# Moving the background's turn behind the copy or sum of each product, and gated splits behind the last copy and sum

## The chip, the cores and the metric

The kernel runs on one core of one Trainium2 chip. The metric is the device time of one execution in microseconds (us); lower is better. A core has engines with a queue of instructions each: TensorE (PE in the profile) multiplies matrices, VectorE (DVE) and ScalarE (ACT) work on tiles, GpSimd (POOL) does the same more slowly, and SyncE (SP) here only issues transfers between the memory of the chip and on-chip tiles. The engines run beside one another and wait for each other through semaphores; within one engine, instructions run in the order in which they stand in its queue.

## The reference

One decoder block over 2048 positions of width 1024, in float32. Its mixer has two parts, gated linear attention and a short gated convolution, between one input and one output projection; then comes a gated FFN of width 2816.

```python
h = rmsnorm(x, norm1_g[l])
proj = h @ w_in[l]
...
o = gla_chunked(q, k, v, log_a)
o = rmsnorm(o, gla_norm_g[l]).astype(x.dtype)
o = o * jax.nn.silu(p_g.reshape(bsz, seq, GLA_HEADS, GLA_DV))
...
u = c_c * c_h
o_conv = c_b * causal_depthwise_conv(u, conv_w[l])
mixed = jnp.concatenate([o_gla, o_conv], axis=-1) @ w_out[l]
x = x + mixed
h2 = rmsnorm(x, norm2_g[l])
ffn = (jax.nn.silu(h2 @ w_ffn_gate[l]) * (h2 @ w_ffn_up[l])) @ w_ffn_down[l]
x = x + ffn
return rmsnorm(x, norm_f_g)
```

## The kernel before

The positions are worked on in two halves of 1024, each half two blocks of 512. Almost all of TensorE's time goes into products of 128 x 512 tiles. A `unit` computes a two by two block of output tiles (c11, c12, c21, c22) from a two by two block of weights and of operands with seven products in place of eight, in the manner of Strassen. The names in `PRODUCTS` are pairs of a weight combination (A11, S1, S2, A12, S3, S4, A22) and an operand combination (B11, T1, T2, B21, T3, B22, T4), and below they are P0 to P6 in this order. Each product runs over four slices of the contraction (two or three in FFN down), and each slice takes three matmuls (L460, L461, L462), because a float32 value is split into a rounded high part (an ACT copy, L193) and the rest (a DVE subtraction, L194): high times high, high times low, low times high. A product is so 12 matmuls as a rule. The weights arrive as `raw`, are combined on POOL or DVE (L435), and split into `wq`; operands arrive as `op`.

The products of a unit share accumulators. P0 goes into bank `oa` and is copied to c11 (`copied`, L500, ACT); P1 goes into `ob` and is copied to c22; P2 is added into `oa` and copied to c12; P3 has a bank of its own and is added to c11 (`plus`, L489, DVE); P4 goes on in `oa` and is added to c22; P5 goes on in `ob` and is added to c12; P6 ends `oa`, which is c21. So the next product in a bank cannot start before the copy or the sum of the one before it has read the bank. In FFN down after its first unit all copies are sums into `y`.

Beside these products runs a "background": generators with the work of other parts (operands of the next stage, the gated linear attention, splits of gated values in FFN up), of which one step is traced at a turn. A turn is a call of `tick` (L271). It counts `pace`; on even counts, or while `hurry` is set, it traces one step of the background; `steady`, `hasty` and `ahead` add steps at some counts; while `ordered` is set, in the first units, it does nothing. In `mul` the turn comes after the product's matmuls (L481) and so ahead of its copy or sum in the program.

What stands in the program is not yet the order of an engine's queue: a scheduler places instructions by the program's order and by when their operands are to be ready (`TileContext` at L1634, with a simulated timeline). `behind(marks)` (L158) adds an edge: what is issued within it stands behind the marked instructions where they are on its own engine. `last_out` holds the last copy of L500 and `last_plus` the last sum of L489; the row statistics (`row_stats`, L545) and `kept` (L352) use these marks already.

In FFN up, a pair of units gives a gate and a value, whose product (DVE, L1310) is a gated value (c or sg in the profile's names, t for the differences POOL makes of them). `split_later` (L1321) is put into the background for them: values in `WHOLE` are stored as they are, the others are split by `store_split` (L1331) into `so`, of which there are three buffers, and stored for FFN down. Transfers of the next stage's operands (`op`, L148) and stores (L151) go through SP's one queue: `in_proj(1)`, the second half's input projection, loads its operands from `siB` and `siT`, which the first half's background makes and stores as pairs `hi` and `lo`, and the attention of the first half loads `kq`, `ee`, `vt` and `gt` in the same queue.

Of the kernel before, what the change touches and what calls it, by code (L numbers as in the profile page):

```python
# [53 lines left out]
def tile_hymba_block(ctx, tc, x, xt, win, wa, wgu, wout, wffn, wdown, wdown_first, small, out):  # L54
# [83 lines left out]
    def bank(name="mm"):  # L138
        return ps.tile([P, PB], F32, name=name, tag="mm")

    def tt(name):
        return tp.tile([P, PB], F32, name=name, tag="t")
# [7 lines left out]
    def store(dst, src):  # L150
        return nc.sync.dma_start(dst, src)  # L151

    last_hi, last_lo, raw_loads = [], [], []
    last_out = []
    unit_splits, unsplit, held, last_plus, with_marks = [], [], [], [], []

    @contextmanager
    def behind(marks):  # L158

        with ExitStack() as stack:  # L160
            for m in marks:
                stack.enter_context(tc.issue_after(m.ins))
            yield
# [3 lines left out]
    def queued(eng, issue):  # L167

        with behind([tails[eng]] if eng in tails else []):
            tails[eng] = issue()  # L170
        return tails[eng]
# [18 lines left out]
    def split(src, hi, lo):  # L190
        if ordered:
            return split_in_order(src, hi, lo)
        last_hi[:] = [act.activation(hi, src, AF.Copy)]  # L193
        last_lo[:] = [dve.tensor_tensor(lo, src, hi.bitcast(F32), ALU.subtract)]  # L194
        return last_lo[0]
# [67 lines left out]
    def step():  # L263
        while background:
            try:
                next(background[0])
                return
            except StopIteration:
                background.pop(0)

    def tick():  # L271
        pace[0] += 1
        if ordered:
            return
        if pace[0] % 2 == 0 or hurry:
            step()
            if steady and pace[0] % 4 == 0:
                step()
        elif hasty and pace[0] % 4 == 3:
            step()  # L280
        elif ahead and pace[0] % 4 == 1:
            next(ahead[0], None)
# [114 lines left out]
    def weight_quarter(src):  # L397

        n = src.shape[-1]
        if halves:  # L400
            h = halves.pop()
        else:
            h = wqp.tile([P, 2, PB], F32R, name="wq", tag="wq")
            if n == PB // 2:
                halves.append(h[:, :, n:])
            h = h[:, :, 0:n]
        split(src, h[:, 0, :], h[:, 1, :])
        catch_up()
        return h
# [8 lines left out]
    def unit_weights(src, raw=None, between=(), eng=pool):  # L418
        raw = raw_weights(src) if raw is None else raw
        between = iter(between)  # L420

        def others():
            for job in next(between, ()):
                job()

        n = src.shape[-1]
        a11, a12, a22, a21 = [raw[:, i, :] for i in range(4)]
        s1 = rawp.tile([P, PB], F32, name="s1", tag="s1", bufs=1)[:, 0:n]
        w = {"A11": weight_quarter(a11)}

        def mix(*args):
            if ordered:
                queued(dve, lambda: dve.tensor_tensor(*args))
            else:
                eng.tensor_tensor(*args)  # L435

        mix(s1, a21, a22, ALU.add)
        mix(a21, a11, a21, ALU.subtract)
        mix(a11, s1, a11, ALU.subtract)
        w["S1"] = weight_quarter(s1)  # L440
        others()
        w["S2"] = weight_quarter(a11)
        others()
        w["A12"] = weight_quarter(a12)
        others()
        w["S3"] = weight_quarter(a21)
        others()
        mix(a12, a12, a11, ALU.subtract)
        w["S4"] = weight_quarter(a12)
        others()  # L450
        w["A22"] = a22 if ordered else weight_quarter(a22)
        halves.clear()
        return w

    def product_step(o, w, op, k, first):
        n = len(op)
        c = slice(k * P, (k + 1) * P)
        wh, wl = w[:, 0, c], w[:, 1, c]
        xh, xl = op[k][:, 0, :], op[k][:, 1, :]
        pe.matmul(o[:], wh, xh, start=first and k == 0, stop=False, skip_group_check=True)  # L460
        pe.matmul(o[:], wh, xl, start=False, stop=False, skip_group_check=True)  # L461
        return pe.matmul(o[:], wl, xh, start=False, stop=k == n - 1, skip_group_check=True)  # L462

    def unit(src, ops, into=None, onto=None, raw=None, between=(), rest=None, eng=pool):

        w = unit_weights(src, raw, between, eng)
        unit_splits[:] = last_hi + last_lo
        with behind(unit_splits):  # L470
            for y, o in unsplit:
                split(y[:], o[:, 0, :], o[:, 1, :])
        unsplit.clear()

        def mul(i, o=None):
            first = o is None
            o = bank() if first else o
            n, m = PRODUCTS[i]
            for k in range(len(ops[m])):
                product_step(o, w[n], ops[m], k, first)  # L480
            tick()  # L481
            return o

        def plus(t, o):
            if ordered:
                queued(dve, lambda: dve.tensor_tensor(t[:], o[:], t[:], ALU.add))
            else:
                with behind(held if rest is not None else []):
                    last_plus[:] = [dve.tensor_tensor(t[:], o[:], t[:], ALU.add)]  # L489
            return t  # L490

        def then():
            if rest is not None:
                next(rest)

        def copied(name, o, at):
            if onto is not None:
                return plus(onto[at], o)
            t = tt(name) if into is None else into[at]
            last_out[:] = [act.activation(t[:], o[:], AF.Copy)]  # L500
            return t


        oa = mul(0)
        c11 = copied("c11", oa, (0, 0))
        ob = mul(1)
        c22 = copied("c22", ob, (1, 1))
        mul(2, oa)
        c12 = copied("c12", oa, (0, 1))
        o = mul(3)  # L510
        then()
        plus(c11, o)
        mul(4, oa)
        then()
        plus(c22, oa)
        if rest is not None:
            next(rest, None)
            w["A22"] = weight_quarter(w["A22"])
            held[:] = last_hi + last_lo
            ordered.clear()  # L520
        mul(5, ob)
        plus(c12, ob)
        mul(6, oa)
        if into is not None or onto is not None:
            copied("c21", oa, (1, 0))
        return [(0, 0, c11, False), (1, 1, c22, False), (0, 1, c12, False), (1, 0, oa, True)]

    def settled(c, in_psum):
# [480 lines left out]
    def in_proj(half, ops, raw=None, between=(), rest=None):  # L1009
        def units():  # L1010
            if half == 0:
                yield unit(win[2], ops, raw=raw, between=between, rest=rest)
            for u in range(0 if half else 3, 12):
                yield unit(win[u], ops, eng=pool if half else dve)
# [289 lines left out]
    def ffn_up(half, ops):  # L1304
        for m in range(NF // 2):
            us = unit(wffn[2 * m], ops)
            sg = {(r, j): silu(c, p) for r, j, c, p in us}
            for r, j, c, _ in unit(wffn[2 * m + 1], ops):
                s = sg[r, j]
                dve.tensor_tensor(s[:], c[:], s[:], ALU.mult)  # L1310
            b11, b12, b21, b22 = [sg[r, j] for r in range(2) for j in range(2)]
            t1, t2, t3, t4 = [bt(n) for n in ("t1", "t2", "t3", "t4")]
            for y, p, q in ((t1, b12, b11), (t2, b22, t1), (t3, b22, b12), (t4, b21, t2)):
                pool.tensor_tensor(y[:], p[:], q[:], ALU.subtract)
            values = [("B11", b11), ("B21", b21), ("B22", b22)]
            if half == 1 and m >= LAST_GROUP:
                values.append(("B12", b12))
            values += [("T1", t1), ("T2", t2), ("T3", t3), ("T4", t4)]
            background.insert(0, split_later(s_act[half][m], values))

    def split_later(dst, values):  # L1321

        for n, y in values:
            if n in WHOLE:
                store(dst[n][:], y[:])
        for n, y in values:
            if n not in WHOLE:
                store_split(dst[n], y)
                yield

    def store_split(dst, y):  # L1331
        o = bx[1].tile([P, 2, PB], F32R, name="so", tag="so")
        split(y[:], o[:, 0, :], o[:, 1, :])
        store(dst[:], o[:].bitcast(F32))
# [304 lines left out]
```

## Time and profile before

| | us |
|---|---|
| median of 3 runs | 2064.49 |
| the runs | 2064.49, 2065.36, 2061.48 |
| profiled execution | 2061.84 |
| its span | 2060.1 |
| TensorE busy | 2023.8 |
| DVE, ACT, POOL busy | 1429.7, 971.3, 770.3 |

All times inside the profile are counted from the start of the span. The stages of the span are these: the first half's input projection up to about 240 us; the second half's, with the first half's attention in the background, up to about 560; the output projections, which have matmuls of lines of their own (L1201 to L1204), up to about 785; FFN up of the first half to about 1190, FFN down to about 1430; then FFN up of the second half to about 1835 and FFN down to the end.

A group of the profile gives busy time, mean duration, and the idle time of its engine just before it with what ended it; the view of waits gives the same idle time by waiting line and releasing line (total, times, longest). In the timeline a row gives the start, the duration, engine, line, operation, output and inputs, and in brackets the idle time before it. A row of the view of windows gives the busy time of PE, weight load, DVE, ACT and POOL in a stretch, then the granted clock of TensorE (1 is full speed), the busy share of the DMA engines and GB/s.

### The profile page before, as it was taken

The page shows a single profiled execution, that of the slowest core. Times are in us where ns is not written, and L with a number is a line of the kernel's source. Part 1 is how long each engine was busy: PE and PEld are TensorE (multiplying, and loading weights), DVE is VectorE, ACT ScalarE, POOL GpSimd, SP SyncE. Part 2 cuts the span into 40 slices and gives each one's busy share as a digit, 9 for nine tenths or more (in the row PEclk, how much of TensorE's full clock was granted, in tenths as well). Part 3 has the DMA queues.
Part 4 walks back from the last instruction along what each step waited for, and adds up shares of the span by engine and source line. Part 5 has one row for each costly group of instructions (what it writes and reads, how often), then busy time and mean ns, then how long its engine had stood idle before and what let it go on. Part 6 is the DMA issues. An engine that isn't in the chain of part 4 may idle for free.

```text
span 2060.1 us, 27151 instructions
## 1 busy us (share of the span) xinstructions
PE 2023.8 (98%) x9271; PEld 1663.5 (81%) x9271; DVE 1429.7 (69%) x2185; ACT 971.3 (47%) x1932; POOL 770.3 (37%) x566
## 2 busy tenths in 40 slices
PE   9999999999999999999999999999999999999997
PEld 8778878887888887888888888787888888888786
DVE  7878976559743786677675677766766666667774
ACT  6765455765542344444444552335434443453344
POOL 0000022113102574464564345533644554434544
PEclk9999999999999999999999999999999999999998
DMA  7356796425686873555454676576444434486653
GB/s 260 124 188 212 285 313 189 130 82 166 225 273 228 319 260 128 199 181 206 160 180 147 234 278 248 184 272 260 162 170 164 169 148 169 173 314 222 235 216 126
DMA packets 189739, 422.54 MB, mean 205 GB/s; under 512 B 19904, under 2 KB 65184, under 8 KB 180128
## 3 DMA queue, kind: packets, MB, share of 16 engines
q1 hardware_dynamic: 189600, 420.81, 57.8%
q8 instruction: 73, 1.20, 0.2%
q14 instruction: 66, 0.54, 0.1%
HBM read 276.02 MB, written 144.70 MB: 204 GB/s over the span
## 4 chain that ended last, share of the span: by engine, by line
PE 82%; DVE 8%; DMA 5%; ACT 2%; issue 2%; POOL 1%; SPq 0%; DVEq 0%; ACTq 0%; POOLq 0%
PE mm L460 24%; PE mm L462 23%; PE mm L461 23%; PE mm L1201 2%; PE mm L1202 2%; PE mm L1204 2%; DVE wq L194 1%; DVE op L194 1%; DMA raw<-in_win_dram 1%; DMA op<-shT 1%; DMA op<-siT 1%; DVE h L882 1%; PE a_ps L958 1%; PE mm L744 1%; PE mm L746 1%
## 5 line engine op out<-in xcount | busy, mean ns | idle before, releaser
L460 PE MATMUL mm<-op,wq 128*128 128x512 f32 x2467 | 964.0, 393 | 20.1 <-ACT c L500 8.4
L461 PE MATMUL mm<-op,wq 128*128 128x512 f32 x2467 | 961.2, 390 | 0.4 <-DVE op L194 0.4
L462 PE MATMUL mm<-op,wq 128*128 128x512 f32 x2467 | 950.8, 391 | 1.3 <-DVE wq L194 1.0
L194 DVE TENSOR_TENSOR wq<-raw,wq 128x512 fp32r<-128x512 f32 (+2 forms) x612 | 488.3, 803 | 243.6 <-ACT wq L193 240.8
L193 ACT ACTIVATE wq<-raw 128x512 fp32r<-128x512 f32 (+2 forms) x612 | 355.8, 587 | 590.5 <-PE mm L462 447.5
L460 PEld LDWEIGHTS mm<-op,wq 128*128 128x128 f32 x2467 | 463.9, 188 | 125.6 <-ACT c L500 11.8
L462 PEld LDWEIGHTS mm<-op,wq 128*128 128x128 f32 x2467 | 463.8, 188 | 101.8 <-DVE wq L194 4.6
L461 PEld LDWEIGHTS mm<-op,wq 128*128 128x128 f32 x2467 | 464.1, 188 | 96.0 <-DVE op L194 2.1
L435 POOL TENSOR_TENSOR s<-raw 128x512 f32<-128x512 f32 (+2 forms) x87 | 114.4, 1315 | 449.2 <-DVE wq L194 299.0
L435 POOL TENSOR_TENSOR raw<-raw 128x512 f32<-128x512 f32 (+2 forms) x174 | 227.1, 1310 | 135.9 <-DVE wq L194 126.6
L435 POOL TENSOR_TENSOR raw<-s,raw 128x512 f32<-128x512 f32 (+2 forms) x87 | 111.3, 1280 | 410.3 <-DVE wq L194 372.6
L489 DVE TENSOR_TENSOR y<-mm,y 128x512 f32<-128x512 f32 x185 | 126.8, 687 | 80.0 <-PE mm L462 79.8
L489 DVE TENSOR_TENSOR c<-mm,c 128x512 f32<-128x512 f32 x196 | 134.7, 687 | 68.4 <-PE mm L462 66.3
L1183 POOL TENSOR_TENSOR ssx<-ssx,q 128x512 f32<-128x512 f32 x52 | 76.3, 1482 | 162.3 <-ACT q L1182 162.0
L500 ACT ACTIVATE c<-mm 128x512 f32<-128x512 f32 x198 | 115.7, 587 | 19.5 <-PE mm L462 16.6
L1201 PE MATMUL mm<-op,wq 128*128 128x512 f32 x256 | 100.9, 395 | 0.0
L1202 PE MATMUL mm<-op,wq 128*128 128x512 f32 x256 | 99.9, 390 | 0.0
L193 ACT ACTIVATE wq<-s 128x512 fp32r<-128x512 f32 (+2 forms) x96 | 56.2, 585 | 84.0 <-PE mm L462 79.9
L194 DVE TENSOR_TENSOR wq<-s,wq 128x512 fp32r<-128x512 f32 (+2 forms) x96 | 82.4, 858 | 2.8 <-ACT wq L193 2.1
L194 DVE TENSOR_TENSOR op<-op 128x512 fp32r<-128x512 f32 x94 | 76.6, 844 | 8.7 <-ACT op L193 8.6
L1204 PE MATMUL mm<-op,wq 128*128 128x512 f32 x256 | 80.2, 391 | 0.0
L1396 POOL TENSOR_TENSOR y<-x,y 128x512 f32<-128x512 f32 x32 | 53.7, 1679 | 45.3 <-DVE y L489 45.3
(232 smaller groups left out, 1847.0 us busy)
## 6 DMA issues: line engine op xcount, KB each, us to landing
raw<-in_wffn_dram SPq DMA_DIRECT2D x44, 1024.0 KB, 6.0
sa_B<-so SPq DMA_DIRECT2D x47, 512.0 KB, 4.3
op<-sa_B SPq DMA_DIRECT2D x47, 512.0 KB, 6.9
raw<-in_win_dram SPq DMA_DIRECT2D x22, 1024.0 KB, 5.4
sa_T<-so SPq DMA_DIRECT2D x44, 512.0 KB, 4.5
op<-sa_T SPq DMA_DIRECT2D x44, 512.0 KB, 6.7
raw<-in_wdown_dram SPq DMA_DIRECT2D x24, 768.0 KB, 6.1
sx<-y SPq DMA_DIRECT2D x48, 256.0 KB, 4.0
```

What stands on the lines that cost most here:

```text
L193: last_hi[:] = [act.activation(hi, src, AF.Copy)]
L194: last_lo[:] = [dve.tensor_tensor(lo, src, hi.bitcast(F32), ALU.subtract)]
L435: eng.tensor_tensor(*args)
L460: pe.matmul(o[:], wh, xh, start=first and k == 0, stop=False, skip_group_check=True)
L461: pe.matmul(o[:], wh, xl, start=False, stop=False, skip_group_check=True)
L462: return pe.matmul(o[:], wl, xh, start=False, stop=k == n - 1, skip_group_check=True)
L489: last_plus[:] = [dve.tensor_tensor(t[:], o[:], t[:], ALU.add)]
L500: last_out[:] = [act.activation(t[:], o[:], AF.Copy)]
L1183: pool.tensor_tensor(ssq[:], ssq[:], q[:], ALU.add)
L1201: pe.matmul(o[e, j][:], wh, m[:, 0, :], start=k == 0, stop=False)
L1202: pe.matmul(o[e, j][:], wh, m[:, 1, :], start=False, stop=False)
L1204: pe.matmul(o[e, j][:], wl, ops[k][j][:, 0, :], start=False, stop=k == KD - 1)
```

## The change

In `unit`, `mul` no longer calls `tick`; each of the seven products has its turn after its copy or sum, and after P6 also where nothing is copied. The number of turns of a unit and their counting are the same. In `split_later`, the split and store of a gated value now stand behind the last copy and the last sum issued at that moment: its ACT copy behind the last ACT copy of L500, its DVE subtraction behind the last DVE sum of L489. No arithmetic is changed.

```diff
@@ unit
             for k in range(len(ops[m])):
                 product_step(o, w[n], ops[m], k, first)
-            tick()
             return o
...
         oa = mul(0)
         c11 = copied("c11", oa, (0, 0))
+        tick()
         ob = mul(1)
         c22 = copied("c22", ob, (1, 1))
+        tick()
         mul(2, oa)
         c12 = copied("c12", oa, (0, 1))
+        tick()
         o = mul(3)
         then()
         plus(c11, o)
+        tick()
         mul(4, oa)
         then()
         plus(c22, oa)
+        tick()
...
         mul(5, ob)
         plus(c12, ob)
+        tick()
         mul(6, oa)
         if into is not None or onto is not None:
             copied("c21", oa, (1, 0))
+        tick()
@@ split_later
             if n not in WHOLE:
-                store_split(dst[n], y)
+                with behind(last_out + last_plus):
+                    store_split(dst[n], y)
                 yield
```

Built, the changed kernel has as many instructions on each engine as before, but for two activation table loads fewer on ACT. TensorE's products stand in another order in a few regions only.

## The prediction

> **What bounds the kernel now.** I read the page first (span, busy times, the chain that ended last, the groups), then the waits of TensorE, then stretches of the timeline around each of its longest waits.
>
> ```profile
> span 2060.1 us, 27151 instructions
> PE 2023.8 (98%) x9271; PEld 1663.5 (81%) x9271; DVE 1429.7 (69%) x2185; ACT 971.3 (47%) x1932; POOL 770.3 (37%) x566
> ...
> PE 82%; DVE 8%; DMA 5%; ACT 2%; issue 2%; POOL 1%; SPq 0%; DVEq 0%; ACTq 0%; POOLq 0%
> ...
> L460 PE MATMUL mm<-op,wq 128*128 128x512 f32 x2467 | 964.0, 393 | 20.1 <-ACT c L500 8.4
> ```
>
> TensorE bounds it: busy 2023.8 of 2060.1 us, so 36.3 us is all that any reordering can win. The start of a product (L460) carries 20.1 us of that idle time. The waits of TensorE say for whom:
>
> ```profile
> PE mm L460 <- ACT c L500: 8.4, 7, 2.1
> PE mm L460 <- DVE c L489: 3.9, 5, 1.6
> PE mm L460 <- ACT wq L193: 2.2, 2, 1.8
> PE mm L460 <- DVE y L489: 2.2, 4, 1.2
> ```
>
> Seven waits for a copy and nine for a sum, 14.5 us together, are what this change can reach: the copy (L500, ACT) and the sum (L489, DVE) must be done before the next product that writes the same bank. Only the places where a background instruction stands between are touched, though. Following these sixteen waits through the order of instructions of both kernels, I find the same instructions ahead in three of the copies and seven of the sums: operand splits, a table load and gate work of the foreground, which no turn of the background places. So most of the 36.3 us stays.
>
> **The change, part by part.** It adds and removes no instruction by itself. A turn of the background now comes after the copy or sum of its product, not before it, 7 turns a unit as before, and the scheduler's order of instructions changes in some regions only. Copies with a background instruction directly ahead fall from 28 to 8 and sums from 44 to 37; elsewhere TensorE's order of products is unchanged, in particular through most of the FFN. I take each region.
>
> *FFN up, steady.* 21 of the 28 copies stood behind a split of a gated value (so, L193) that waits for DVE:
>
> ```profile
> ACT so L193 <- DVE c L1310: 35.1, 22, 2.8
> ```
>
> ACT idles 35.1 us there, but TensorE waits in only one of those units, because the copy has a whole product (12 matmuls at 0.23 us, 2.7 us) to be done in. That unit is this one:
>
> ```profile
> 834.32 0.68 DVE L1310 TENSOR_TENSOR c<-c,c 128x512 f32<-128x512 f32 x1
> 835.03 0.63 ACT L193 ACTIVATE so<-c 128x512 fp32r<-128x512 f32 x1 [2.75 <-DVE c L1310]
> 835.57 0.58 ACT L500 ACTIVATE c<-mm 128x512 f32<-128x512 f32 x1
> 836.20 0.50 PE L460 MATMUL mm<-op,wq 128*128 128x512 f32 x1 [1.19 <-ACT c L500]
> ```
>
> The copy could have run 2.75 us earlier; after, it stands ahead of the split: **-1.2** (bounds -1.2 and 0, if another split takes the place). The other 21 cost 0 now and 0 after. The split's two edges to the last copy and sum delay the stores of the gated values by at most about a product, 2.7 us; these are read back only a group later in FFN down, except the last group's, taken next.
>
> *First unit of FFN down, both halves.* A DVE sum stands behind three subtractions of `so`:
>
> ```profile
> 1837.40 0.91 DVE L194 TENSOR_TENSOR so<-sg,so 128x512 fp32r<-128x512 f32 x1
> 1838.24 0.68 DVE L194 TENSOR_TENSOR so<-c,so 128x512 fp32r<-128x512 f32 x1
> 1838.84 0.68 DVE L194 TENSOR_TENSOR so<-t,so 128x512 fp32r<-128x512 f32 x1
> 1839.44 0.68 DVE L489 TENSOR_TENSOR y<-mm,y 128x512 f32<-128x512 f32 x1
> 1840.17 0.50 PE L460 MATMUL mm<-op,wq 128*128 128x512 f32 x1 [1.20 <-DVE y L489]
> ...
> 1197.60 0.50 PE L460 MATMUL mm<-op,wq 128*128 128x512 f32 x1 [0.69 <-DVE y L489]
> ```
>
> After, the subtractions are spread between sums. Waits of 0.69 and 1.20 go; I leave 0.2 of each for the one subtraction that may remain ahead: **-1.5** (bounds -1.9 and 0). A copy in the second half's FFN up (0.7 us at 1503) has two more matmuls as cover, 0.46 us: **-0.4** (bounds -0.7 and 0).
>
> *First half's input projection, 100 to 135 us.* The largest single item:
>
> ```profile
> 120.78 1.28 ACT L1005 ACT_TABLE_LOAD   x1
> ...
> 124.03 0.61 ACT L193 ACTIVATE wq<-raw 128x512 fp32r<-128x512 f32 x1
> ...
> 122.45 0.39 PE L462 MATMUL mm<-op,wq 128*128 128x512 f32 x1
> 124.69 0.50 PE L460 MATMUL mm<-op,wq 128*128 128x512 f32 x1 [1.85 <-ACT wq L193]
> ...
> 126.77 0.63 PE L460 MATMUL mm<-op,wq 128*128 128x512 f32 x1
> 127.19 0.63 PE L461 MATMUL mm<-op,wq 128*128 128x512 f32 x1
> ...
> 126.00:130.00 4.00, 4.00 (x14) 3.25 (x13) 3.40 (x9) 2.13 (x4) 0.00 (x0) 0.57 0.34 131
> ```
>
> A weight split stands behind the table load and the squares of the row statistics, TensorE waits 1.85 us, and right after it the granted clock is 0.57 over four microseconds: matmuls 0.42 us apart for about 8 of them, 0.2 us each too much, 1.6 us. After, this table load is gone (two of ACT's loads go, 1.28 us each; ACT is 47% busy, so they count only here), the split comes earlier, and both go: -3.5. But two pairs of dependent products, P4 and P6 of a unit, then follow each other in one bank with nothing between. The nearest row of such a pair:
>
> ```profile
> 488.05 0.39 PE L1127 MATMUL o_ps<-carry,kq 128*128 128x128 f32 x2
> 488.48 0.68 DVE L489 TENSOR_TENSOR c<-mm,c 128x512 f32<-128x512 f32 x1
> 489.21 0.50 PE L460 MATMUL mm<-op,wq 128*128 128x512 f32 x1 [0.78 <-DVE c L489]
> ```
>
> End of the last matmul (0.39 after its start), 0.05 to the sum, 0.68, 0.05 to the matmul, less the normal 0.23 step: 0.95 us each, +1.9. Net **-1.6** (bounds -3.5, if the pairs find other work between, and +1.9, if the split is still late).
>
> *195 to 225 us.* DVE is the full engine here:
>
> ```profile
> 180.00:225.00 45.00, 44.71 (x198) 36.73 (x197) 44.96 (x74) 22.97 (x45) 0.00 (x0) 1.00 0.72 241
> ```
>
> DVE is busy 44.96 of 45.00 us, and TensorE still idles only 0.3. Two new pairs, P2 and P4, come with two matmuls between: 0.95 - 0.45 = 0.5 each; the 0.3 us wait for a copy goes: **+0.7** (bounds -0.3, and +3.2 with each pair at the longest wait for such a sum, 1.6).
>
> *Where the second half's input projection begins.* SP's queue and transfers set this stretch:
>
> ```profile
> 243.09 1.68 SPq L148 DMA_DIRECT2D op<-siB  x3
> 244.83 0.42 SPq L148 DMA_DIRECT2D kq<-sk  x1
> 246.06 0.32 SPq L151 DMA_DIRECT2D siB<-lo  x1
> 246.66 0.32 SPq L151 DMA_DIRECT2D siT<-t  x1
> ...
> 242.00:249.00 7.00, 7.00 (x32) 5.82 (x31) 7.00 (x10) 2.60 (x5) 3.30 (x2) 1.00 0.78 240
> 249.00:278.00 29.00, 26.89 (x118) 21.64 (x117) 21.93 (x37) 15.61 (x31) 2.89 (x2) 1.00 1.01 383
> ...
> 273.45 1.25 ACT L193 ACTIVATE op<-op 128x512 fp32r<-128x512 f32 x2 [1.90 <-DMA op<-siT]
> ...
> 275.75 1.14 ACT L193 ACTIVATE op<-op 128x512 fp32r<-128x512 f32 x2
> 276.79 0.58 ACT L500 ACTIVATE c<-mm 128x512 f32<-128x512 f32 x1
> ...
> 277.42 0.50 PE L460 MATMUL mm<-op,wq 128*128 128x512 f32 x1 [2.11 <-ACT c L500]
> ```
>
> The DMA engines are full (share 1.01) from 249 to 278, and an operand split waits on a transfer. After, the stores of `siB` and `siT` and more small `kq` loads (0.4 us of queue each) stand in SP's queue ahead of the first three operand loads, which so start after 246.66, not at 243.09: 3.6 us later. The engines' free share before 249 takes 1.5 of it back (7 us at 1 - 0.78), which leaves +2.1; one more operand split (0.57 each in the row of two) ahead of the copy at 276.79 gives +0.5. The wait of 2.1 us becomes 4.7; whether the clock halves behind it is even, since 1.85 us was followed by it and 2.11 us was not: half of 1.6, +0.8. **+3.4** (bounds 0, if the other loads in flight hide it, and +5.8: 3.6, 0.6 and 1.6).
>
> Sum: -1.2 - 1.5 - 0.4 - 1.6 + 0.7 + 3.4 = -0.6 us. The profiled execution took 2061.84 us and the median of the runs is 2064.49, 2.65 above it, within their spread of 3.9 us; on the median the forecast is **2063.9 us**.
>
> The Trainium skill, "TensorE: Matmul & The Clock Gate", Part 1, says that the clock falls to half after an idle activity window of about 3.4 us, on windows that run freely, and its part on oscillation that gaps up to that length are harmless. The trace differs: 1.85 us of waiting was enough once. By the rule, the halving at 126 would not belong to that wait.
>
> **The rivals.** *DVE's full stretch gives way (slower, 0.20).* Between 180 and 240 the sums of some 20 products pass a DVE queue without a gap. If the new order lets a weight subtraction of 1.4 us slip ahead of a sum whose product has no cover, TensorE waits that long. It decides against the change from four such sums (4 x 1.4 = 5.6, against the -1.3 of the other terms); with six, 8.4 - 1.3 = +7.1, 2071.6. Against it: the count of sums behind the background falls. *The operand loads come as late as their issue (slower, 0.10).* 5.8 in place of 3.4, and the next product also waits for its operand, 3.6 more; with the -4.0 of the other terms +5.4, 2069.9. It decides from 8.1 us at this place. The full DMA share speaks for it, the idle share before 249 against. *Nothing new is late (faster, 0.22).* The loads hide (0), the pairs find cover (-3.5, -0.3), and the other three go whole: -3.5 - 0.3 - 1.2 - 1.9 - 0.7 = -7.6, 2056.9; with the pairs at half, 2058.5. *The change doesn't act (0.08):* the large waits have foreground work ahead and the terms cancel, 2064.5. *The halving is no child of the wait (0.08):* the 1.6 stays at some other place and falls due in full behind 4.7 us of waiting: -0.6 + 1.6 + 0.8 = +1.8, 2066.3; that the 2.11 us wait went without it speaks for it. This is the time by the skill's rule above.
>
> **How the numbers follow.** The forecast itself has 0.32. About 0.2%, 4.1 us, is what a measurement of this kernel can tell. Faster by that: most of the third rival and a little of the forecast's own spread, 0.24. Slower: most of the first two and a little of the rest, 0.29. Within: 0.47. For the range I leave out the far ends of the first and third rival and take 2057.5 to 2070.5; the forecast's own range is 2060 to 2068.
>
> **What would show it.** Right: ACT's waits of `so` for L1310 no longer precede a copy; no TensorE wait at 835, and about 0.2 at 1197 and 1840; the clock at 1.0 from 123 to 130, with two new waits of about 1 us for DVE c L489 between 100 and 135; the first operand loads of the second half issued after 246.7 and waits of some 4 to 5 us near 277; table loads of L540 and L1005 at 6 and 0. Wrong: new waits for L489 in 180 to 240 above 1 us in all, a wait near 277 that didn't grow or grew past 6, or new halvings of the clock.

## The result, and the profile after

The changed kernel takes 2066.32 us (median of 22 runs, 2061.61 to 2069.63). The kernel before, timed beside it, takes 2062.76 us (22 runs, 2059.5 to 2066.2). The ratio is 1.0017, with a 95% interval of 1.0011 to 1.0023: 3.6 us slower. The time lies in the forecast's range, but the forecast of -0.6 us has the wrong sign. The profiled execution of the changed kernel took 2068.62 us.

The page of the changed kernel:

```profile
span 2066.9 us, 27121 instructions
PE 2029.3 (98%) x9271; PEld 1664.0 (81%) x9271; DVE 1428.3 (69%) x2185; ACT 968.1 (47%) x1930; POOL 766.2 (37%) x566
...
L460 PE MATMUL mm<-op,wq 128*128 128x512 f32 x2467 | 965.3, 393 | 19.2 <-ACT c L499 5.1
...
L462 PE MATMUL mm<-op,wq 128*128 128x512 f32 x2467 | 951.0, 391 | 2.6 <-DVE wq L194 2.2
```

TensorE's idle time barely grew, from 36.3 to 37.6 us, but its busy time grew by 5.5 us for the same 9271 matmuls. Two more periods of a halved clock (below) are some 3 us of that. Its waits (line, what ended it, total, times, longest) changed places. The copy is L499 here and the sum L488:

```profile
PE mm L460 <- ACT c L499: 5.1, 6, 1.8
PE mm L460 <- DVE c L488: 4.7, 6, 1.6
PE mm L460 <- ACT op L193: 3.3, 2, 2.1
PE mm L460 <- DMA op<-siB: 2.9, 3, 2.3
PE mm L462 <- DVE wq L194: 2.2, 6, 0.8
```

Waits for a copy fell from 8.4 to 5.1 us, for `y` sums from 2.2 to 0.3. In their place stand 2.9 us for a transfer of operands, which before did not appear, 3.3 for an operand split (1.4 before) and 2.2 for the low part of a weight (1.0 before).

Both traces hold the same number of matmuls, so the start of the n-th can be compared. The difference of the two, taken between the same matmuls, gives the time gained or lost in a stretch of the span. For the profiled execution of the changed kernel, stretches in us of the kernel before. These are the stretches of which this text speaks; each of the others gains or loses 0.7 us at most:

| stretch | after, against before | what is in it |
|---|---|---|
| 63 to 91 | +1.6 | the clock halved behind a wait that both have |
| 91 to 137 | -1.6 | wait of 1.85 and halved clock gone, two new waits of 0.8 |
| 182 to 262 | +0.7 | DVE's full stretch |
| 262 to 332 | +4.3 | operands of the second half, and a halved clock |
| 763 to 790 | +1.3 | the clock halved behind a wait that both have |
| 790 to 842 | -1.5 | the wait of 1.2 for the copy |
| 1184 to 1208 | +0.7 | first unit of FFN down, first half |
| 1490 to 1515 | -0.1 | the wait of 0.7 for the copy at 1503 |
| 1827 to 1844 | -0.3 | first unit of FFN down, second half |
| whole | +6.9 | |

**Where the second half's operands are loaded.** The timeline of the changed kernel, SP's issues and then TensorE's first matmuls after a wait:

```profile
241.85 2.79 SPq L148 DMA_DIRECT2D kq<-sk  x4
246.08 0.32 SPq L151 DMA_DIRECT2D siB<-lo  x1
...
248.01 1.27 SPq L148 DMA_DIRECT2D op<-siB  x3
...
254.72 3.17 SPq L148 DMA_DIRECT2D vt<-sv  x3
258.88 1.80 SPq L148 DMA_DIRECT2D gt<-sg  x3
261.69 1.60 SPq L148 DMA_DIRECT2D op<-siT  x2
...
265.28 2.15 SPq L148 DMA_DIRECT2D op<-siB  x3
...
272.92 0.47 PE L460 MATMUL mm<-op,wq 128*128 128x512 f32 x1 [2.27 <-DMA op<-siB]
...
282.00 1.01 PE L460 MATMUL mm<-op,wq 128*128 128x512 f32 x2 [2.14 <-ACT op L193]
```

The window of the same kernel right after (busy times, then the granted clock 0.60):

```profile
282.00:286.00 4.00, 4.00 (x10) 2.96 (x11) 2.29 (x4) 2.12 (x5) 0.68 (x1) 0.60 1.02 380
```

Before, the first operand loads were issued at 243.09, the first of T2 at 256.78 (`op<-siT` x2) and of B21 at 261.19 (`op<-siB` x3). Now they are issued at 248.01, 261.69 and 265.28, and ahead of the first load of T2 stand thirteen small loads (four `kq`, two `ee`, four `vt`, three `gt`) where eight stood before. The old wait of about 2.1 us is still there, at 282; one of 2.27 us for the transfer stands ahead of it, and behind the last of them the clock is 0.60.

**The clock.** Two further halvings stand behind waits that are in both kernels. The stretch after the wait at 82, of the kernel before and of the changed one:

```profile
84.00:88.00 4.00, 4.00 (x18) 3.29 (x19) 3.72 (x7) 3.93 (x9) 0.00 (x0) 1.00 0.77 223
```
```profile
84.00:88.00 4.00, 3.92 (x12) 3.04 (x12) 3.74 (x8) 2.95 (x6) 0.00 (x0) 0.61 0.69 203
```

In four microseconds 18 matmuls before and 12 after, for the same wait of TensorE (1.9 us, for ACT wq L180) ahead of them. The profiled execution of the changed kernel has three such stretches (85, 282, 781), that of before one (126). Two more of about 1.5 us make some 3 of the 6.9 us between the two profiled executions; what is left, about 3.9, is near the 3.6 us between the medians.

### The profile page after: what moved, and what is told of

It reads as the page before. It is cut to its first block, busy times and chain, and to the rows that moved or that the text cites. A ratio compares the mean times of both kernels' runs of the same rounds, so it can differ in the third digit from the quotient of the medians.

```text
span 2066.9 us, 27121 instructions
## 1 busy us (share of the span) xinstructions
PE 2029.3 (98%) x9271; PEld 1664.0 (81%) x9271; DVE 1428.3 (69%) x2185; ACT 968.1 (47%) x1930; POOL 766.2 (37%) x566
## 4 chain that ended last, share of the span: by engine, by line
PE 85%; DVE 7%; DMA 3%; ACT 2%; issue 2%; POOL 0%; SPq 0%; DVEq 0%; ACTq 0%; POOLq 0%
PE mm L460 25%; PE mm L462 24%; PE mm L461 24%; PE mm L1207 2%; PE mm L1208 2%; PE mm L1210 2%; DVE op L194 2%; DVE wq L194 1%; DMA op<-shT 1%; PE a_ps L964 1%; DVE h L888 1%; PE mm L750 1%; PE mm L752 1%; PE mm L751 1%; PE o_ps L1131 1%
## 5 line engine op out<-in xcount | busy, mean ns | idle before, releaser
L488 DVE TENSOR_TENSOR c<-mm,c 128x512 f32<-128x512 f32 x196 | 134.7, 687 | 75.6 <-PE mm L462 72.1
L488 DVE TENSOR_TENSOR y<-mm,y 128x512 f32<-128x512 f32 x185 | 126.8, 687 | 79.8 <-PE mm L462 79.1
L499 ACT ACTIVATE c<-mm 128x512 f32<-128x512 f32 x198 | 115.7, 588 | 58.0 <-PE mm L462 54.8
L194 DVE TENSOR_TENSOR wq<-s,wq 128x512 fp32r<-128x512 f32 (+2 forms) x96 | 75.0, 781 | 3.6 <-ACT wq L193 3.6
L1316 DVE TENSOR_TENSOR c<-c,c 128x512 f32<-128x512 f32 x66 | 70.6, 1069 | 0.1
```

## The experiments

Theory A is that the loss is made where the second half's operands are loaded. The rivals: it is made in FFN down (B), or it is nothing but the number of halved clock periods (C). Times are medians; each run was timed beside the kernel before, and its ratio is to that.

**The late turn in one stage alone, and everywhere else.** In both, `turn` stands at both places and a flag says which one acts (this moves the lines of `unit` by up to 7).

```diff
+    late_turn = [True]
+    def turn(late):
+        if late == late_turn[0]:
+            tick()
...
     in_proj(0, ops, raw, between, rest)
+    late_turn[0] = False          # e1, which has no edges on the splits
```

> The kernel before, with the late turn in the first half's input projection alone; the FFN, its splits and the rest as before. Theory A (the loss is made where the second half's operands are loaded: operand loads issued behind stores and small loads): the whole loss is here, +3 to +4 us on the median, and the profile has the first operand loads issued at about 248 us and waits of about 2.3 and 2.1 us at 270 to 282. Theory B (the loss is made in FFN down, where weight subtractions now stand behind the gated splits): +0 to +1 us here. Theory C (the loss is only a larger number of halved clock periods): 0 to +1.5 us, with a count of halvings that has nothing to do with the place of the edit.

Measured: 2066.63 us against 2062.19, ratio 1.0023 (1.0015 to 1.0032). The late turns of the first half's input projection alone make the whole loss. The stretch from 262 to 332 costs +3.3, with these waits:

```profile
272.09 0.47 PE L466 MATMUL mm<-op,wq 128*128 128x512 f32 x1 [1.36 <-DMA op<-siB]
...
281.11 0.98 PE L466 MATMUL mm<-op,wq 128*128 128x512 f32 x2 [2.14 <-ACT op L193]
```

```diff
+    late_turn[0] = False
     in_proj(0, ops, raw, between, rest)
+    late_turn[0] = True           # e2, with the edges on the splits
```

> The changed kernel, with the early turn kept in the first half's input projection alone. Theory A: the loss goes, -1 to +0.5 us against before, operand loads first issued at about 243 us. Theory B: +2 to +4 us stay, with the waits of L462 for DVE wq at about 1190 and 1830. Theory C: between.

Measured: 2060.03 us against 2062.19, ratio 0.9993 (0.9984 to 1.0001). The loss is gone; the same stretch is at -1.7. B and C both fall as the main cause: everything in the FFN is as in the changed kernel here, and the profile has two halved stretches (84, 774) without being slow.

**One part of the change alone.**

```diff
                 if n not in WHOLE:
-                store_split(dst[n], y)
+                with behind(last_out + last_plus):     # e3, turns as before
+                    store_split(dst[n], y)
```

> The kernel before, with the gated splits behind the last copy and sum, the turns as before. By the prediction's own step the wait of 1.2 us at 835 goes and those in the first units of FFN down (0.7 and 1.2 us) shrink: -1 to -3 us. Theory B: these come back as waits for a weight subtraction, 0 to +1 us. Theory A and C: within 1 us of before, operand loads of the second half as before.

Measured: 2070.13 us against 2062.19, ratio 1.0036 (1.0023 to 1.005), from 7 runs of 2064.11 to 2071.81. None of the theories had expected a loss of this size. The wait at 835 did go. What came in its place can be read from the waits of this kernel:

```profile
PE mm L462 <- DVE wq L194: 4.3, 8, 1.3
```

The low part of a weight takes 4.3 us of waiting where it took 1.0, in the first units of FFN down among others (1.5 us in each, at 1196 and 1845). There are also a wait of 1.8 us for a weight split at 1397, a longer wait behind the row statistics at 1701 (2.6 us, 0.7 before) and four halved stretches, two of them behind these two waits. The profiled execution lost 9.9 us, some 6.5 of them in the FFN; which part of it every execution pays is not settled.

> The changed kernel without the edges on the gated splits: only the turns are late. Theory A: as slow as the changed kernel or 1 us slower, +3 to +5 us. Theory B: about +2 us less than the changed kernel, since the splits stand where they were by the program's order: +0 to +2 us.

This is the changed kernel with `store_split` outside of `behind`. Measured: 2066.4 us against 2062.19, ratio 1.0018 (1.0009 to 1.0026): as slow as the changed kernel, as A says. And the wait at 835 is still there:

```profile
839.81 0.63 ACT L193 ACTIVATE so<-c 128x512 fp32r<-128x512 f32 x1 [2.76 <-DVE c L1316]
840.35 0.58 ACT L499 ACTIVATE c<-mm 128x512 f32<-128x512 f32 x1
...
840.98 0.50 PE L460 MATMUL mm<-op,wq 128*128 128x512 f32 x1 [1.20 <-ACT c L499]
```

So it is the edge that moves this split behind the copy. The late turns alone leave it ahead.

**The order of the loads alone.** In the kernel before, the first operand load was put behind the last two stores of the operands made ahead. The scheduler then put the six `kq` and `ee` loads ahead of them too.

```diff
+                if (n, k, e) == ("B21", 3, 1):
+                    last_store.append(y)        # and the store of T4, k = 3
...
+            for p in src[n]:
+                with behind(marks):             # last_store for the first load, then nothing
+                    ops[n].append((load_whole if n in WHOLE else load_pair)(p))
```

> The kernel before, with one edge more: the second half's first operand load stands in SP's queue behind the stores of the last B21 and T4 of the operands made ahead, and with it the four kq and two ee loads come ahead of the operand loads, as in the changed kernel; no turn and no split is moved. Theory A (late operand loads make the loss): +3 to +5 us, first operand load issued at about 247 us, waits of 2 us or more at 270 to 282. Rival (the products' new order and the pairs without cover make it): 0 to +1 us.

Measured: 2063.34 us against 2061.1, ratio 1.001 (1.0001 to 1.0019): +2.2 us, about six tenths of the loss. SP's issues of this kernel:

```profile
246.57 1.86 SPq L148 DMA_DIRECT2D op<-siB  x4
...
254.45 1.44 SPq L148 DMA_DIRECT2D op<-siT  x2
...
261.11 1.65 SPq L148 DMA_DIRECT2D op<-siB  x3
```

The first loads are 3.5 us late (4.9 in the changed kernel, whose TensorE is itself about 1 us behind there), but those of T2 and B21 come no later than before (254.45 and 261.11, against 256.78 and 261.19), and there is no wait for a transfer at 272. The stretch costs +0.8, and a halved clock at 277, some 1.6 us, is in it. So late first loads alone do not make the wait for the transfer. What makes the +2.2 us on the median isn't shown: in this profile TensorE's waits from 262 to 290 are 2.6 us against 2.1. In the other direction, the changed kernel with the small loads moved:

```diff
     def load_pair(src):
-        load(o[:].bitcast(F32), src[:])
+        op_loads.append(load(o[:].bitcast(F32), src[:]))
...
             for i, r in enumerate(src):
-                load(dst[:, i, :], r[:, s])
+                with behind(op_loads[7:7+1] if (b, t) == (0, 0) else []):
+                    load(dst[:, i, :], r[:, s])
```

> The changed kernel, with the first small loads of the attention (kq, ee, vt, gt) behind the eighth operand load of the second half; the two stores still stand ahead of the operand loads. Theory A with the small loads as the main part: 1.5 to 3 us of the changed kernel's loss come back (+0.5 to +2 us against before). With the two stores as the main part: less than 1 us comes back.

Measured: 2060.81 us against 2061.1, ratio 0.9996 (0.9987 to 1.0005). One edge on small loads takes the whole loss back, with all turns late and all gated splits behind their marks. The operand loads and TensorE's only wait for a transfer:

```profile
244.21 2.36 SPq L148 DMA_DIRECT2D op<-siB  x4
...
258.18 0.32 SPq L148 DMA_DIRECT2D op<-siT  x1
...
261.75 1.39 SPq L148 DMA_DIRECT2D op<-siB  x2
...
273.01 0.50 PE L461 MATMUL mm<-op,wq 128*128 128x512 f32 x1 [0.26 <-DMA op<-siB]
```

The loads of T2 and B21 are 3.5 us earlier than in the changed kernel, and the wait for the transfer falls from 2.27 to 0.26 us. SP mostly waits, between its issues, for an earlier operand load, and once for a weight load. These rows are those of the changed kernel from 240 to 276:

```profile
SPq L148 <- DMA op<-siT: 6.1, 7, 1.4
SPq L148 <- DMA op<-siB: 5.7, 7, 1.4
SPq L151 <- DMA raw<-in_win_dram: 1.4, 1, 1.4
```

The traces show why. The 1236 transfers of SP's queue take eight semaphores in turn, and in all 13 traces of the block's kernels no issue starts before the transfer eight places ahead of it has landed, whatever its size. So a small load of 64 KB holds one of eight places, as an operand load of 512 KB does. Both delays of the changed kernel come out of this:

- Four `kq` loads now stand ahead of the last store of `siB`, which is so exactly eight places behind a weight load (`raw`). That landed at 246.02, the store was issued at 246.08, and the first operand loads behind it at 248.01. In e6 no small load is there, the store is issued at 242.50 and the first operand load at 244.21.
- The first load of T2 stands eight places behind an operand load that landed at 261.62, and was issued at 261.69. Six small loads (`vt`, `gt`) are among the seven between them, and four of the six waited 0.7 to 1.4 us each for an earlier operand load to land.

How much each delay costs by itself isn't shown, since e6 takes both away.

**Turns without edges, and the rest.**

> Late turns everywhere but in the first half's input projection, no edges on the gated splits. Theory A: -2 to 0 us against before. If the edges on the splits help only beside late turns, it is 0 to 1 us slower than the same kernel with them (2060.0 us); if they cost by themselves, it is faster than that.

Measured: 2061.18 us against 2061.1, ratio 1.0 (0.9991 to 1.0009). The same kernel with the edges (e2) is at 0.9993, and the intervals overlap; that the edges help beside late turns is not shown. This profile shows something else. The wait for the weight split at 124 is there as it was before, and the clock stays at 1.00:

```profile
123.00:126.00 3.00, 1.35 (x7) 0.98 (x8) 1.86 (x8) 2.98 (x7) 0.00 (x0) 1.00 0.28 117
126.00:130.00 4.00, 4.00 (x21) 3.33 (x19) 3.85 (x9) 2.73 (x5) 0.00 (x0) 1.00 0.34 131
```

In the eight experiments that keep this place as before (e2, e3, e5, e7, e9 to e12) the clock never halves there, behind gaps of 1.97 to 2.0 us between matmuls. In the one profiled execution that the prediction was made from, it did, behind 2.01 us.

**Is a halving a matter of chance?** A program of its own asks this:

```diff
+    for r in range(REPEATS):                        # 24
+        for g in range(len(LENGTHS)):               # (0, 2, 4, 6, 8, 10, 13, 16)
+            for i in range(m):                      # 38 to 48 matmuls into one bank
+                pe.matmul(o[:], t[:] if i == 0 else x1[:, 0:P], x1[:], ...)
+            act.activation(t[:], o[:, 0:P], AF.Copy, scale=1e-3)
+            for i in range(k):                      # k of LENGTHS
+                act.activation(t[:], t[:].bitcast(F32), AF.Copy)
```

> Another program: 192 bursts of 38 to 48 matmuls of 128x512, and behind each a chain of 1 to 17 ACT copies on which the next burst waits, in eight lengths of 24 each (the outputs are zeros, nothing of the block is computed). Theory C (a halving of the clock follows a gap by chance, the chance growing with the gap's length): gaps of 0.8 us none, of 1.8 to 2.2 us some of the 24, of 3.4 us and more nearly all. Rival (a halving needs a gap of 3.4 us): none below 3.4 us.

Measured, from the start times of the matmuls: a gap is the distance of two matmuls less 0.227 us, and it counts as halved where at least three matmuls of the next 26 stand some 0.43 us apart.

| gap, us | gaps | halved |
|---|---|---|
| 0.6 | 23 | 0 |
| 1.3 | 24 | 0 |
| 1.95 to 2.25 | 24 | 4 |
| 2.6 | 24 | 17 |
| 3.3 | 24 | 17 |
| 4.0 to 6.3 | 72 | 72 |

Behind the four gaps of 1.95 us there are 7 or 8 slow matmuls, at 0.2 us each some 1.5 us. The rival falls: halvings come well below 3.4 us, and they come behind some gaps of a length and not behind others, 4 of 24 at about 2 us and 17 of 24 at 2.6. In all the profiles of the block's kernels taken together (without their last 30 us, where few matmuls follow), gaps of 1.75 to 2.25 us were followed by one in 19 cases of 60, those of 1.4 to 1.75 us in none of 25. Of the 60 cases, those at about 83 us (2.09 us) had 9 halvings in 13, those at 775 (1.95) 6 in 13, those at 126 (2.0) 1 in 9, those at 1430 (1.85) none in 13; whether the place counts beside the length isn't shown.

**Could the gains be had without the loss?**

> The kernel before, with the first small loads of the attention behind the eighth operand load. If what the small loads cost is their place among the transfers in flight, the wait of 2.1 us at 277 shrinks here too: -1 to -2.5 us. If they only matter beside the late turns: within 1 us of before.

This is the edge of e6 put into the kernel before. Measured: 2062.6 us against 2061.16, ratio 1.0005 (0.9996 to 1.0013). No gain: the wait of 2.1 us at 277 is a wait for the copy behind operand splits, and at 1.7 us it is still there. My expectation missed this.

> Late turns and gated splits everywhere but in the first half's input projection, and the small loads behind the eighth operand load. If both gains add up: -2 to -4 us against before, the fastest of all. If the first was the chance of the clock: -0.5 to -1.5 us.

Measured: 2060.91 us against 2061.16, ratio 0.9996 (0.9987 to 1.0005). The gains don't add up.

> Late turns and the edges on the gated splits in the FFN alone, everything ahead of it as before. By the prediction's steps in the FFN: -3.1 us. By the profile of the changed kernel (the wait at 835 gone, -1.5; the first unit of FFN down slower by 0.7 in the first half and faster by 0.5 in the second; others of both signs): -1.5 to +1 us.

Here `late_turn` is set at the FFN. Measured: 2060.0 us against 2061.16, ratio 0.9994 (0.9986 to 1.0003). Stretch by stretch: -1.5 at 790 to 842, 0.0 at 1184 to 1208, -0.3 at 1827 to 1844. What the change does in the FFN is worth the wait at 835 and little else.

> The kernel before, with the gated splits behind the last copy alone, not behind the last sum; the turns as before. If the edge on DVE's subtraction made the 7.9 us of the run with both edges: within 1.5 us of before. If the edge on ACT or the changed order as such made it: +4 to +9 us again.

`behind(last_out)` in place of `behind(last_out + last_plus)`. Measured: 2063.53 us against 2061.16, ratio 1.0011 (1.0002 to 1.002): +2.4 us, between the two expectations. By the medians the edge on DVE's subtraction makes the larger part of e3's 7.9 us, the edge on ACT or the new order some of it. This profile has the wait for a weight split near 1397 (2.2 us at 1393), but not the one at 1701.

No version was shown to be faster than the kernel before: the lowest ratios (e2, e11, e6, e10) have intervals that reach 1.

## Why the prediction was right or wrong

The forecast on the median was -0.6 us; measured was +3.6. Two steps of it failed: the halved clock behind the wait at 124, booked as a cost of that wait, and the gain in the first unit of FFN down. Term by term, against the stretches of the changed kernel's profile:

- **100 to 135 us, -1.6: wrong, and a large part of the miss.** The pairs cost 0.8 each where 0.95 was forecast, and the wait of 1.85 went. But the forecast also took off 1.6 us for the halved clock behind that wait. The profile agrees by the letter (-1.6), but that is luck, and nothing was won: of nine profiles that keep this wait, only the one that the prediction was made from has a halving there. In the other eight this stretch is at -1.6 too, without any change to it. Against them the place is worth 0.
- **195 to 225 us, +0.7: right.** The stretch costs +0.7 in the changed kernel, and in e1, e4 and e6, which have the late turns there too. Two starts of a product behind a copy, at 199 and 219, are 0.5 us late each, and the one at 215 is gone.
- **Operands of the second half, +3.4: right in place and size.** +4.3 in the changed kernel, +3.3 and +5.6 in e1 and e4. The wait for a transfer came ahead of the old one, not in it (2.27 and 2.14 us, 4.4 in all, where 4.7 was forecast), and the clock halved behind the old one in all three. Inside the term the reason was incomplete: the prediction priced the first loads by the stores ahead of them and took time back for the free share of the DMA engines. It is the small loads that hold the places in the queue, and with them the store of `siB` and the loads of T2.
- **The wait at 835, -1.2: right.** -1.5. It takes the edge; late turns alone do nothing (e4).
- **First unit of FFN down, -1.5: wrong.** The waits for the sum of `y` did go (0.3 us are left in all), but +0.7 and -0.3 were measured. The +0.7 is that of one execution: e2, e6, e10 and e11, with the same order of DVE's instructions there, have 0.0, which is still no gain. The prediction said that the subtractions are spread between the sums and left 0.2 us for one of them; it did not ask what else stands behind them in DVE's queue. It is the low part of a weight (DVE, then TensorE of the changed kernel; in e11 two matmuls behind such subtractions start 0.3 and 0.4 us late, together about the 0.69 that went):

```profile
1196.23 1.18 DVE L194 TENSOR_TENSOR so<-c,so 128x512 fp32r<-128x512 f32 x1
1197.33 0.68 DVE L1316 TENSOR_TENSOR sg<-mm,sg 128x512 f32<-128x512 f32 x1
1197.93 0.41 DVE L194 TENSOR_TENSOR wq<-raw,wq 128x256 fp32r<-128x256 f32 x1
...
1198.40 0.50 PE L462 MATMUL mm<-op,wq 128*128 128x512 f32 x1 [0.82 <-DVE wq L194]
```

- **The copy at 1503, -0.4: about right in mechanism** (0.4 of 0.7 us of waiting is left), too small to be seen.

With 0 for the first and +0.4 for the fifth (0.7 - 0.3), the sum is 0 + 0.7 + 4.3 - 1.5 + 0.4 - 0.1 = +3.8, near the +3.6 that was measured; with 0.0 - 0.3 for the fifth it is +3.1. So the sign was lost by two terms, 1.6 and 1.2 to 1.9 us: a halving of the clock that other executions don't have, and a wait that was traded for another.

Of the rivals, late operand loads ended on the right side, at a lower price than the +5.4 given. DVE's full stretch did not give way. "The halving is no child of the wait" is borne out in one half: the 1.6 us were not to be gained there. Its 2066.3 us is the measured time by luck, since it starts from a median of three runs that lies 1.7 us above that of the 22; as a difference it says +1.8, where +3.6 was measured. The rule of the Trainium skill, "TensorE: Matmul & The Clock Gate", Part 1 (an idle window of about 3.4 us, windows that run freely), was set against one halving behind 1.85 us, and I took the trace's side. The gap program shows both in part. Free windows agree with halvings that come by chance, and every gap of 4.0 us and more had one. But a gap need not be 3.4 us: 17 of 24 at 2.6 us were followed by one.

## What to carry to other kernels

Before a slow stretch is charged to the wait in front of it, look for the same wait elsewhere in the trace: if it is not always followed by the slow clock, charge it by its chance, not in full. When work is moved in the program, the queue of transfers moves too: see which small loads now stand ahead of large ones, since in this queue each holds one of eight places, and put the small ones behind the large ones with an edge. Where a sum or copy is freed from an instruction, name what else waits behind that instruction on its engine.

## What the runs showed of the hardware that was not expected

TensorE's clock can halve behind a wait of 2 us, for about 7 or 8 matmuls of 0.43 us each, 1.5 us, but only sometimes: 4 of 24 gaps of 2 us, 17 of 24 of 2.6 us, 17 of 24 of 3.3 us, all of 72 from 4.0 us on, none of 47 up to 1.3 us. The profiles of the block's kernels had six to eleven gaps of 1.4 to 2.8 us each (without the last 30 us), and none to four halvings. At some 1.5 us each that is, as an estimate, enough for differences of several us between executions without any difference in the program.
